# Tiles of split weights that begin at eight places of SBUF modulo 512 bytes instead of one

## The chip, the core and the metric

The kernel runs on one core of a Trainium2 chip. The metric is the device time of one execution in microseconds (us). A core has a matrix engine (TensorE: PE for its matmuls, PEld for the loads of its stationary operand), a vector engine (DVE), an activation engine (ACT), GpSimd (POOL), a queue engine (SP) and 16 DMA engines. They share SBUF, a memory of 128 partitions; a tile of `[128, n]` floats takes 4n bytes at one address in every partition. All addresses below are bytes within a partition.

## The reference

A trunk of two layers over 256 tokens of width 1024, in float32. Each layer adds half a SwiGLU (width 2816), an attention mixer and half a second SwiGLU, each on an RMS-normed input:

```python
h = rms_norm(x, ffn1_norm[layer])
x = x + 0.5 * swiglu(h, ffn1_w_gate[layer], ffn1_w_up[layer], ffn1_w_down[layer])
h = rms_norm(x, mix_norm[layer])
x = x + even_mixer(...)   # layer 0: global and windowed attention;  layer 1: odd_mixer, a neighbourhood
h = rms_norm(x, ffn2_norm[layer])
x = x + 0.5 * swiglu(h, ffn2_w_gate[layer], ffn2_w_up[layer], ffn2_w_down[layer])
```

A last norm follows. Nearly all of the work is products of 256 rows with large weight matrices, each of which is read once.

## The kernel before

**Split products.** A float32 weight W is split into a high part, W rounded to float32r, and a low part, W minus the high part. The activations are split likewise. A product is then three matmuls in float32r (`mm`, L474 to L476): activation high by weight high, activation high by weight low, activation low by weight high. The activation (a 128 by 128 block of `th`, `tl`, `g_h`, `g_l` and the like) is the stationary operand, which a load (LDWEIGHTS, shown as PEld) brings in ahead of each matmul; the weight part (512 columns of `hi` or `lo`) is the moving operand that streams past it. A row `s<-hi,th` is thus a matmul into the PSUM bank `s`, with `hi` moving and `th` stationary.

**The supply of weights.** Weights arrive by DMA in the tiles `raw` (three buffers of 8192 bytes). ACT makes the high part of up to 1024 columns (`high_part`, L482, `hi<-raw`), DVE then the low part (`low_part`, L485, `lo<-raw,hi`: two inputs in SBUF). `supply` (L422 on) takes a pair of tiles for that from the pool `wp`, which holds seven `hi` and seven `lo`, so that up to seven splits lie ready ahead of the matmuls. Splits of sums of weights (`shi`, `slo`, kind "sum") have buffers of their own in the phase pool, three each.

**The order of the work** is written out by the kernel itself: each matmul calls `tick`, which steps waiting tasks and supplies a split when a rate says that it is due. The change doesn't touch any of this.

**Places in SBUF.** Pools lie behind each other: `one` (x, the transposed activations `th` and `tl`, constants), `raw`, `wp`, `two` (small tiles), and behind these the pools of each phase (`g_h`, `g_l`, `shi`, `slo`, attention tiles). The tiles that matmuls and splits read are whole multiples of 512 bytes, and `one` begins so that they start at 128 modulo 512: x at 4224, `th` at 12416, `raw` at 28800, the seven `hi` at 53376 + 4096 n, the seven `lo` at 82048 + 4096 n. The first small tile of `two` is `mhalf`, a constant of `FILLER` columns of which at most eight are read; at 96 columns its end is at 111104, and with it the phase pools begin at 113280, which is 128 modulo 512 as well. A block of a stationary operand is 512 bytes and a moving one 2048 bytes, so that every matmul of 512 columns reads both of its operands from 128 modulo 512 on. That place is called the common one here.

Of the kernel before, what the change touches and what calls it, by code (L numbers as in the profile page):

```python
# [9 lines left out]
F32 = mybir.dt.float32  # L10
F32R = mybir.dt.float32r
# [7 lines left out]
P = 128  # L19
# [103 lines left out]
AHEAD_START = 8  # L123
FIRST = [1, 1, 2, 2, 2]

FILLER = 96
HALF = [slice(0, HD), slice(HD, P)]

ROW = 224
# [6 lines left out]
class Split:  # L136
# [3 lines left out]
    def __init__(self, raw, uses, last=False, narrow=False, kind="wp", then=None):  # L140
        self.raw, self.last, self.narrow, self.kind, self.then = raw, last, narrow, kind, then
        n = raw.shape[1]
        self.left = sum(uses[i % len(uses)] for i in range(n))
        self.parts, self.made = None, 0
# [64 lines left out]
class Trunk:  # L209
# [4 lines left out]
    def __init__(self, ctx, tc, a, out):  # L214
        self.ctx, self.tc, self.nc, self.a, self.out = ctx, tc, tc.nc, a, out
        pool = lambda name, bufs, **kw: ctx.enter_context(tc.tile_pool(name=name, bufs=bufs, **kw))
        self.one = pool("one", 1)
        self.ph = None
        self.raw = pool("raw", RAWS)
        self.wp = pool("wp", FIT["wp"])  # L220

        self.two = pool("two", 2)
        self.acc = pool("acc", 1, space=PSUM)
        self.n = 0
        self.rate = RATE[0]
        self.tasks, self.last, self.last_v = [], [], [[], []]
        self.units, self.whole, self.queue, self.due, self.half = self.plan(), [], [], 0, None
        self.live = {kind: 0 for kind in FIT}
        self.ahead = len(FIRST) - RAWS

        self.hts = {}

    def name(self, s):
        self.n += 1
# [185 lines left out]
    def supply(self):  # L420

        self.low()  # L422
        if not self.whole:
            return
        split = self.whole[0]
        _, a, w = split.raw.shape
        if split.parts is None:
            if split.kind == "wp":
                split.parts = [self.wp.tile([P, 2, 512], F32R, tag=n, name=self.name(n)) for n in ("hi", "lo")]
            else:  # L430
                split.parts = [self.t([P, 2, 512], n, FIT["sum"], F32R) for n in ("shi", "slo")]
            split.parts = [t[:, :a, :w] for t in split.parts]
            self.live[split.kind] += 1
        sl = slice(split.made, split.made + split.step())
        self.high_part(split.parts[0][:, sl], split.raw[:, sl])
        split.made = sl.stop
        self.half = (split, sl)
        if split.made == a:
            self.whole.pop(0)
# [1050 lines left out]
    def run(self):  # L1490
# [7 lines left out]
        def warm(n):  # L1498
            for _ in range(n):
                nc.tensor.matmul(nothing, zero16[:, :P], zero16, start=True, stop=True)  # L1500

        self.warm = warm
        warm(WARM)
        self.mhalf = self.little([P, FILLER], "mhalf")
        nc.gpsimd.memset(self.mhalf, -0.5)
# [73 lines left out]
```

## Time and profile before

| what | value |
|---|---|
| time, median of two runs | 935.4 us (935.3 to 935.5) |
| profiled execution, its own time | 935.71 us |
| its span, first to last instruction | 933.7 us |
| granted TensorE clock, mean | 0.999 |
| busy: PE, DVE, ACT, POOL | 921.5, 773.4, 675.9, 92.6 us |
| instructions on PE | 4405 |
| `hi` by ACT (L482) | 372 instructions, 320.1 us |
| `lo` by DVE (L485) | 372 instructions, 377.7 us |

The span is the stretch in which instructions ran; the execution's own time is 2.0 us longer. The end of a matmul in the profile is modelled and overlaps the next one, so the length of a matmul in a row (0.39 us) is not what it costs. What a stream of matmuls costs is read from the distance between their starts.

### The profile page before, as it was taken

The numbers are of one execution on the slowest core, as the hardware profiler recorded it, in microseconds if no ns is written. First come the engines' busy times: TensorE is split into PE (matmuls) and PEld (weight loads), VectorE is DVE, ScalarE is ACT, GpSimd is POOL, SyncE is SP. The second block draws the span as 40 slices with busy tenths as digits, with TensorE's granted clock in tenths as the row PEclk, the third lists the DMA queues.
The fourth block names the chain that finished last, engine by engine and source line by source line (L and its number), as shares of the span: only waits on it lengthen the run. The fifth ranks groups of instructions, "written<-read, shape, count | busy, mean of one in ns | idle before, by whom it ended". The sixth has DMA issues, their size and how long they took to land.

```text
span 933.7 us, 12374 instructions
## 1 busy us (share of the span) xinstructions
PE 921.5 (99%) x4405; PEld 754.3 (81%) x4405; DVE 773.4 (83%) x1198; ACT 675.9 (72%) x1084; POOL 92.6 (10%) x152
## 2 busy tenths in 40 slices
PE   9999999999999999999999999999999999999997
PEld 6887888877778888888888888888878888888885
DVE  6799679778868889799878888978867696977898
ACT  7778876467777778885657879657777586778853
POOL 1300000064420000000100000008030000000001
PEclk9999999999999999999999999999999999999999
DMA  8857865644327577757466787566434367588651
GB/s 297 283 172 256 244 213 184 218 142 109 112 92 231 173 237 236 233 191 265 156 193 211 216 278 207 225 210 200 155 99 159 105 204 225 168 265 254 164 212 53
DMA packets 129341, 183.14 MB, mean 196 GB/s; under 512 B 50688, under 2 KB 63744, under 8 KB 129280
## 3 DMA queue, kind: packets, MB, share of 16 engines
q1 hardware_dynamic: 128704, 181.58, 61.8%
q8 instruction: 34, 0.56, 0.2%
q10 hardware_dynamic: 576, 0.79, 0.2%
q14 instruction: 27, 0.22, 0.1%
HBM read 169.76 MB, written 1.05 MB: 183 GB/s over the span
## 4 chain that ended last, share of the span: by engine, by line
PE 88%; DVE 7%; ACT 3%; issue 1%; POOL 0%; POOLq 0%; ACTq 0%; DVEq 0%
PE s L476 13%; PE s L475 13%; PE s L474 12%; PE pj L474 12%; PE pj L475 11%; PE pj L476 11%; DVE lo L485 3%; PE o L474 2%; PE o L476 2%; PE o L475 2%; PE o L1053 2%; PE tp L1130 1%; ACT hi L482 1%; PE tp L530 1%; PE tp L474 1%
## 5 line engine op out<-in xcount | busy, mean ns | idle before, releaser
L485 DVE TENSOR_TENSOR lo<-raw,hi 128x1024 fp32r<-128x1024 f32 (+1 forms) x372 | 377.7, 1034 | 81.8 <-ACT hi L482 80.2
L482 ACT ACTIVATE hi<-raw 128x1024 fp32r<-128x1024 f32 (+1 forms) x372 | 320.1, 892 | 53.9 <-PE s L476 12.6
L474 PE MATMUL s<-hi,th 128*128 128x512 f32 x378 | 148.1, 392 | 0.0
L475 PE MATMUL s<-lo,th 128*128 128x512 f32 x378 | 147.2, 389 | 0.2 <-DVE lo L485 0.2
L476 PE MATMUL s<-hi,tl 128*128 128x512 f32 x378 | 147.2, 390 | 0.0
L474 PE MATMUL pj<-hi,th 128*128 128x512 f32 x366 | 146.2, 399 | 0.0
L475 PE MATMUL pj<-lo,th 128*128 128x512 f32 x366 | 143.2, 391 | 0.6 <-DVE lo L485 0.4
L476 PE MATMUL pj<-hi,tl 128*128 128x512 f32 x366 | 142.8, 390 | 0.0
L475 PEld LDWEIGHTS s<-lo,th 128*128 128x128 f32 x378 | 71.0, 188 | 15.0 <-DVE lo L485 0.5
L476 PEld LDWEIGHTS s<-hi,tl 128*128 128x128 f32 x378 | 70.9, 188 | 14.9
L474 PEld LDWEIGHTS s<-hi,th 128*128 128x128 f32 x378 | 71.0, 188 | 14.5
L475 PEld LDWEIGHTS pj<-lo,th 128*128 128x128 f32 x366 | 68.9, 188 | 15.2 <-DVE lo L485 2.6
L476 PEld LDWEIGHTS pj<-hi,tl 128*128 128x128 f32 x366 | 68.7, 188 | 14.5
L474 PEld LDWEIGHTS pj<-hi,th 128*128 128x128 f32 x366 | 68.8, 188 | 14.0 <-issue 1.0
L494 POOL TENSOR_TENSOR rstd<-var,mhalf 128x1 f32<-128x1 f32 (+2 forms) x16 | 17.1, 1070 | 586.6 <-ACT th L515 309.7
L563 ACT COPY turned<-glu 128x1024 uint16<-128x1024 uint16 (+1 forms) x48 | 60.2, 1253 | 13.2 <-DMA glu<-turned 13.2
L559 ACT COPY turned<-glu 128x1024 uint16<-128x1024 uint16 (+1 forms) x48 | 46.3, 965 | 24.1 <-DVE glu L797 16.3
L482 ACT ACTIVATE shi<-raw 128x1024 fp32r<-128x1024 f32 x28 | 29.6, 1059 | 32.7 <-DVE raw L398 23.0
L474 PE MATMUL s<-hi,g_h 128*128 128x512 f32 (+1 forms) x134 | 52.5, 392 | 0.0
L476 PE MATMUL s<-hi,g_l 128*128 128x512 f32 (+1 forms) x134 | 52.0, 388 | 0.0
L475 PE MATMUL s<-lo,g_h 128*128 128x512 f32 (+1 forms) x134 | 52.0, 388 | 0.0
L482 ACT ACTIVATE shi<-two 128x1024 fp32r<-128x1024 f32 x28 | 29.6, 1058 | 23.8 <-DVE two L398 23.7
(350 smaller groups left out, 1657.3 us busy)
## 6 DMA issues: line engine op xcount, KB each, us to landing
raw<-in_ffn_w_down SPq DMA_DIRECT2D x44, 1024.0 KB, 5.1
raw<-in_ffn_w_up SPq DMA_DIRECT2D x28, 1024.0 KB, 5.1
raw<-in_ffn_w_gate SPq DMA_DIRECT2D x26, 1024.0 KB, 5.3
raw<-in_ffn_w_gate SPq DMA_DIRECT2D x35, 512.0 KB, 4.2
raw<-in_ffn_w_up SPq DMA_DIRECT2D x32, 512.0 KB, 5.2
raw<-in_odd_w_qkv SPq DMA_DIRECT2D x12, 1024.0 KB, 5.2
raw<-in_even_w_in SPq DMA_DIRECT2D x4, 1024.0 KB, 5.1
raw<-in_even_w_out SPq DMA_DIRECT2D x8, 512.0 KB, 5.7
```

Of the source, the lines that this page charges most:

```text
L474: mm(ps, h, wh, start=first, stop=False)
L475: mm(ps, h, wl, start=False, stop=False)
L476: mm(ps, l, wh, start=False, stop=last)
L482: self.nc.scalar.activation(hi, src, AF.Copy)
L485: self.nc.vector.tensor_tensor(lo, src, hi.bitcast(F32), op=ALU.subtract)
L494: nc.gpsimd.tensor_tensor(r[:, :n], v[:, :n], self.mhalf[:, :n], op=ALU.pow)
L530: nc.tensor.transpose(tb[:, j * P : (j + 1) * P], self.x[tt][:, b * P : (b + 1) * P], self.ident)
L559: self.nc.scalar.copy(planes.rearrange("p (h c) -> p h c", h=2), back.rearrange("p (c h) -> p h c", h=2))
L563: self.nc.scalar.copy(planes.rearrange("p (c h) -> p h c", h=2), back.rearrange("p (h c) -> p h c", h=2))
L1053: self.nc.tensor.matmul(O[64 * s : 64 * s + 64, i * P : i * P + P], v(b0 + i, s, kc), pT[s][:, i, kc, :], start=(kc == 0), stop=(kc == 1),)
L1130: nc.tensor.transpose(tb[:, o : o + P], p[:, i, kc * P : kc * P + P], self.ident)
```

## The change: what it does

`hi` tiles get eight columns more than are used (1032 floats, 4128 bytes), so that each of the seven begins 32 bytes later modulo 512 than the one before it. Between the last `hi` and the first `lo` lies a new tile `apart` of 32 bytes, to which nothing is written; the seven `lo` tiles keep their size. `mhalf` shrinks from 96 to 32 columns, by as many bytes as the others have gained (7 x 32 + 32 = 256), so that everything behind it stays where it was.

| tile | before, modulo 512 | after, modulo 512 |
|---|---|---|
| `hi`, the seven | 128 each | 128, 160, 192, 224, 256, 288, 320 |
| `lo`, the seven | 128 each | 384 each |
| `raw`, x, `th`, `tl`, `g_h`, `g_l`, `shi`, `slo` | 128 | 128 |

The instructions of every engine, their order, their sizes and their waits are the same, apart from the memset of `mhalf`, which writes 32 columns for 96.

```diff
-FILLER = 96
+FILLER, STEP = 32, 8
...
-        self.hts = {}
+        self.hts, self.apart = {}, []
...
             if split.kind == "wp":
-                split.parts = [self.wp.tile([P, 2, 512], F32R, tag=n, name=self.name(n)) for n in ("hi", "lo")]
+                hi = self.wp.tile([P, 1024 + STEP], F32R, tag="hi", name=self.name("hi"))
+                if not self.apart:
+                    self.apart.append(self.wp.tile([P, STEP], F32, tag="apart", name=self.name("apart"), bufs=1))
+                lo = self.wp.tile([P, 2, 512], F32R, tag="lo", name=self.name("lo"))
+                split.parts = [hi[:, :1024].rearrange("p (a w) -> p a w", a=2), lo]
             else:
                 split.parts = [self.t([P, 2, 512], n, FIT["sum"], F32R) for n in ("shi", "slo")]
```

## The prediction

> **What bounds the kernel now.** I read the page first, its busy times and its chain of work, then PE's waits, then the starts of single matmuls in the timeline. From the page:
>
> ```profile
> span 933.7 us, 12374 instructions
> PE 921.5 (99%) x4405; PEld 754.3 (81%) x4405; DVE 773.4 (83%) x1198; ACT 675.9 (72%) x1084; POOL 92.6 (10%) x152
> ...
> PE 88%; DVE 7%; ACT 3%; issue 1%; POOL 0%; POOLq 0%; ACTq 0%; DVEq 0%
> PE s L476 13%; PE s L475 13%; PE s L474 12%; PE pj L474 12%; PE pj L475 11%; PE pj L476 11%; DVE lo L485 3%; PE o L474 2%; PE o L476 2%; PE o L475 2%; PE o L1053 2%; PE tp L1130 1%; ACT hi L482 1%; PE tp L530 1%; PE tp L474 1%
> ```
>
> PE has work nearly all the time and the chain lies on it for 88%. Of the instructions whose addresses change, DVE's `lo` holds 3% of the chain and ACT's `hi` 1%. What PE itself waited for, longest first:
>
> ```profile
> PE o L1500 <- DVE zeros L1494: 1.4, 1, 1.4
> ...
> PE pj L475 <- DVE lo L485: 0.4, 2, 0.2
> PE o L475 <- DVE lo L485: 0.3, 2, 0.2
> ...
> PE s L475 <- DVE lo L485: 0.2, 1, 0.2
> ```
>
> PE's waits for `lo` sum to 0.9 us (its weight loads add a few more), so that the supply of weights is in time. What is left to gain is the distance between matmuls. Timeline of a stretch inside a feed-forward stage (start, length, engine, line):
>
> ```profile
> 399.36 1.05 ACT L482 ACTIVATE shi<-two 128x1024 fp32r<-128x1024 f32 x1
> ...
> 399.58 0.39 PE L474 MATMUL s<-hi,g_h 128*128 128x512 f32 x1
> 399.58 0.19 PEld L475 LDWEIGHTS s<-lo,g_h 128*128 128x128 f32 x1
> 399.81 0.39 PE L475 MATMUL s<-lo,g_h 128*128 128x512 f32 x1
> 399.81 0.19 PEld L476 LDWEIGHTS s<-hi,g_l 128*128 128x128 f32 x1
> ...
> 400.49 0.39 PE L475 MATMUL o<-lo,g_h 128*128 128x512 f32 x1
> ...
> 401.17 0.39 PE L475 MATMUL pj<-lo,g_h 128*128 128x512 f32 x1
> ...
> 401.25 0.62 ACT L559 COPY turned<-glu 128x512 uint16<-128x512 uint16 x1 [0.85 <-DVE g_l L485]
> 401.39 0.39 PE L476 MATMUL pj<-hi,g_l 128*128 128x512 f32 x1
> ```
>
> From 399.58 to 401.39 there are eight distances in 1.81 us, 0.226 us each. ACT was at work until 400.41 and idle from then to 401.25 (its row gives 0.85 us of idle time); the three distances from 400.49 to 401.17, in that gap, are 0.227 us each. A busy neighbour thus costs PE nothing here. The next stationary load starts together with the running matmul: both operands are read at once, and both from the common place.
>
> Matmuls of 384 columns, near the end:
>
> ```profile
> 924.91 0.33 PE L474 MATMUL s<-hi,g_h 128*128 128x384 f32 x1
> ...
> 925.95 0.22 PE L474 MATMUL tp<-hi,g_h 128*128 128x128 f32 x1
> ```
>
> Six distances lie in 1.04 us, 0.1733 us each. Against 0.2265 us for 512 columns, 128 columns cost about 53 ns, 0.415 ns a column, and about 14 ns of every matmul don't depend on its length. That is all that a better place could save on PE: a stream that met another's bank again and again along its way would cost by the column.
>
> **The change part by part.** All durations are of the one profiled execution, which took 935.71 us by itself and 933.7 us as a span; the median of the two timed runs is 935.4 us, 0.3 us less, and the sum is made on that.
>
> *Matmuls on moved tiles.* Counted in the built program, 3696 matmuls have 512 columns; 2240 read `hi`, 1120 `lo`, 336 `shi` or `slo`. One `hi` tile in seven keeps its place (316 matmuls), so 2240 - 316 + 1120 = 3044 read from a new one. Before, none of the 3696 had its operands at different places, so the price has to be bounded. The nearest row in which both reads go on at once is a run of transposes of `x` (moving: the identity, stationary: a block of `x`, both from the common place):
>
> ```profile
> 448.55 0.60 PE L530 MATMUL tp<-mats,x 128*128 128x128 f32 x4
> 448.55 0.35 PEld L530 LDWEIGHTS tp<-mats,x 128*128 128x128 f32 x3
> ...
> L530 PE MATMUL tp<-mats,x x80: 270/272/328, 181.2 to 754.0; 128*128 128x128 f32 x80
> ```
>
> Four of them take 0.60 us to the end of the last, whose length is 0.272, so three distances are 0.33 us: 109 ns. At twice the 0.415 ns (these are plain float32) 128 columns are 106 ns, so that only some 3 ns are left over, with the loads beside them. If meeting at one place cost a fixed 14 ns, it should stand here too. I therefore hold the 14 ns to belong to a float32r matmul and not to its place, and take 0. The bounds: below, 14 - 3 = 11 ns less for each of 3044, -33 us; above, the slowest steady stretch of such matmuls, in the even mixer:
>
> ```profile
> 215.50 0.39 PE L475 MATMUL pj<-lo,th 128*128 128x512 f32 x1
> ...
> 216.42 0.39 PE L476 MATMUL pj<-hi,tl 128*128 128x512 f32 x1
> ```
>
> Four distances in 0.92 us, 230 ns or 3.5 ns over the usual, with single ones of 0.24 (10 ns over): +11 us, at the farthest +30 us.
>
> *ACT's and DVE's splits.* Minimum, median and maximum in ns, of the tiles that move (two sizes mixed) and of those that stay (one size):
>
> ```profile
> L482 ACT ACTIVATE hi<-raw x372: 609/1044/1105, 6.2 to 915.2; 128x1024 fp32r<-128x1024 f32 x102, 128x512 fp32r<-128x512 f32 x84
> L485 DVE TENSOR_TENSOR lo<-raw,hi x372: 670/1217/1435, 6.9 to 916.5; 128x1024 fp32r<-128x1024 f32 x102, 128x512 fp32r<-128x512 f32 x84
> ...
> L482 ACT ACTIVATE shi<-raw x28: 1044/1062/1067, 53.8 to 910.9; 128x1024 fp32r<-128x1024 f32 x28
> L485 DVE TENSOR_TENSOR slo<-raw,shi x28: 1217/1220/1227, 54.8 to 912.0; 128x1024 fp32r<-128x1024 f32 x28
> ```
>
> From the smallest `lo` of 512 columns (670) to the median of 1024 (1217) the difference is 547 ns for 512 columns, about 1.07 ns a column, though both inputs and the output lie at the same place: no sign that two streams get in each other's way. A row whose places do differ says the same:
>
> ```profile
> L1142 DVE TENSOR_TENSOR t<-pj,gtab x10: 280/282/692, 225.5 to 238.5; 128x128 f32<-128x128 f32 x8, 128x512 f32<-128x512 f32 x2
> ...
> L1142 DVE TENSOR_TENSOR t<-pj,gtab 128x128 f32<-128x128 f32 x8 | 1.8, 281 | 0.0
> ```
>
> The eight of 128 columns write the four quarters of a head's 64 columns (`times(t2[:, :, o], ...)`), which begin 0, 64, 128 and 192 bytes behind the tile's start. Their smallest is 280 and their mean 281, so place moves DVE by no more than a few nanoseconds. So 0 for both. Bounds, on the chain's share alone (3% and 1% of 933.7, 28 and 9 us): all `lo` as long as the longest (1435 against 1217, 18%) and all `hi` at 1105 against 1044 (6%) give +5.6 us; at best each becomes as short as the shortest of its size (1044 against 1062, 1.7%, and 1217 against 1220, 0.2%), which gives -0.2 us. What covers such growth is the seven splits that lie ready; without that cover, PE would wait for each `lo` directly.
>
> The Trainium skill, "SBUF — State Buffer", section "Who interferes with whom", says that engines get in each other's way only at the ports that DVE and GpSimd share, and that PE and ACT never wait for anyone. PE's distances above agree with it. For ACT the rows leave it open (1044 to 1067 for one size in fixed places). By the rule alone the sum is 0 as well.
>
> *`mhalf`.* Its memset is one instruction at the start:
>
> ```profile
> L1505 POOL MEMSET mhalf<- x1: 177/177/177, 0.7 to 0.7; 128x96 f32 x1
> ```
>
> It can become 0.1 us shorter at most, and it runs while PE waits for DVE's zeros. 0.
>
> Sum: 935.4 + 0 + 0 + 0 = 935 us.
>
> **The rivals.** *Faster: the 14 ns are a collision of the two reads.* Each matmul would lose up to 11 ns where its moving operand begins elsewhere: 3044 x 11 ns = 33 us, 902 us. For it: every matmul in the trace has both operands at the same place, so the trace can't refute it. Against it: the transposes, and that the reads run at different speeds (2048 bytes against 512 in one matmul), so that wherever they begin the one must pass the other. It decides from 18.7 / 3044 = 6.1 ns a matmul. The Trainium skill, "TensorE: Matmul & The Clock Gate", section "Back-to-back issue gap", gives N / 2.4 + 2.5 ns for a stream, 216 ns at 512 columns, where this trace has 226.5; by it some 10 ns here would be foreign to a matmul, which would favour this case.
>
> *Slower: streams that begin off the common place cost PE.* Now both reads start in step and never vary; moved apart, or begun at an odd multiple of 32 bytes, a moving read might be held up more often, as some matmuls in the mixers are. At 7 ns a matmul (between the 3.5 and the 10 of the mixer's rows) it is 3044 x 7 = 21 us, 957 us. The point is again 6.1 ns. For it: the mixers show that distances above 226 ns exist. Against it: they stand only where matmuls of other shapes are mixed in.
>
> *No change, but DVE becomes later.* In the stretch with the densest DVE (busy us of PE, PEld, DVE, ACT and POOL; then PE, PEld and DVE on `lo` alone):
>
> ```profile
> 370.00:440.00 70.00, 70.00 (x311) 57.96 (x310) 61.62 (x76) 52.42 (x65) 0.00 (x0) 1.00 0.72 238
> 370.00:440.00 70.00, 35.36 (x92) 17.08 (x91) 32.78 (x29) 1.00 0.72 238
> ```
>
> Of 70 us DVE works 61.62, 32.78 of them on `lo`. `lo` would have to grow by 8.38 / 32.78 = 26% before DVE had no slack here; the longest row allows 18%. So this stays inside the bound of +6 us, 941 us.
>
> *The change does nothing that it says* is excluded as to the places, which the built program has as the table shows; that they don't matter is the forecast.
>
> **How the numbers follow.** A measurement of this kernel is taken to tell 2% (18.7 us) from no change. No change to speak of, with the splits' bounds and up to 3 ns a matmul on either side: 0.83, of which 0.05 for a later DVE. The collision that goes: 0.10. The moved streams that cost: 0.07. The likeliest case's own range is 935 - 0.2 - 9 to 935 + 5.6 + 9, 926 to 950; since an effect of 3 ns on every matmul is already unlikely and the upper bounds don't add up at once, I cut its upper end to 946 and give the lower end to 922, towards the likelier rival. Outside lie then the two rivals and a little of the rest, 0.2.
>
> **What would show it.** Right: the distance in the feed-forward stages stays 0.226 us, `hi` and `lo` keep their medians of 1044 and 1217, the span stays within some us of 933.7. The faster rival shows as distances of 0.215 to 0.220 on `lo` matmuls and on six `hi` tiles in seven, with the 384 columns at 0.162; the slower one as 0.23 and more, different from tile to tile; a later DVE as more than 0.9 us of PE's waits for `lo`. A changed distance would make the prediction wrong, for nothing else has the size.

## The result: slower by 1.4%, outside the range

The changed kernel takes 948.66 us (948.5 to 948.83) against 935.4 us: a ratio of 1.0142, 95% interval 1.0098 to 1.0185, 13.3 us. The profiled execution took 948.83 us, its span is 946.8 us, 13.1 us longer than before. The page after:

```profile
span 946.8 us, 12374 instructions
PE 935.1 (99%) x4405; PEld 754.9 (80%) x4405; DVE 774.1 (82%) x1198; ACT 677.1 (72%) x1084; POOL 91.6 (10%) x152
...
PE 88%; DVE 6%; ACT 3%; issue 1%; DMA 0%; POOL 0%; POOLq 0%; ACTq 0%; DVEq 0%
```

PE is still the bound, with 13.6 us more of busy time; DVE and ACT are as they were. Their splits have not moved either (L489 and L486 are L485 and L482 of before):

```profile
L486 ACT ACTIVATE hi<-raw x372: 612/1044/1107, 6.4 to 928.2; 128x1024 fp32r<-128x1024 f32 x102, 128x512 fp32r<-128x512 f32 x84
L489 DVE TENSOR_TENSOR lo<-raw,hi x372: 673/1215/1431, 7.1 to 929.6; 128x1024 fp32r<-128x1024 f32 x102, 128x512 fp32r<-128x512 f32 x84
```

Nor does PE wait more for `lo`; it was 0.9 us before:

```profile
PE o L479 <- DVE lo L489: 0.3, 2, 0.2
```

What has grown is the distance between matmuls. The same matmuls of a feed-forward stage in the timeline after, two stretches of it:

```profile
402.03 0.40 PE L478 MATMUL s<-hi,g_h 128*128 128x512 f32 x1
402.26 0.39 PE L479 MATMUL s<-lo,g_h 128*128 128x512 f32 x1
...
404.13 0.39 PE L478 MATMUL pj<-hi,g_h 128*128 128x512 f32 x1
...
409.70 0.39 PE L478 MATMUL pj<-hi,g_h 128*128 128x512 f32 x1
...
411.74 0.40 PE L478 MATMUL o<-hi,g_h 128*128 128x512 f32 x1
```

From 402.03 to 404.13 there are nine distances of 0.233 us. From 409.70 to 411.74 there are nine of 0.227 us, as before the change: there the trace, set beside the program, has a `hi` tile at 128 modulo 512, the one that did not move, with its `lo` at 384. Over the trace, the distances behind matmuls of 512 columns (those under 260 ns, some 3575 in each) have a mean of 227.36 ns before and 231.25 ns after, 3.9 ns more. 3575 x 3.9 ns = 13.9 us: that is the whole loss. In a window of 170 us without mixers (busy us and count of PE), before and after:

```profile
440.00:610.00 170.00, 170.00 (x759) 1.00 0.69 213
```

```profile
440.00:610.00 170.00, 170.00 (x745) 1.00 0.66 207
```

Fourteen matmuls fewer fit into it, 1.8%. This count is used below for the other kernels.

### The profile page after: what moved, and what is told of

It reads as the page before. It is cut to its first block, busy times and chain, and to the rows that moved or that the text cites. A ratio compares the mean times of both kernels' runs of the same rounds, so it can differ in the third digit from the quotient of the medians.

```text
span 946.8 us, 12374 instructions
## 1 busy us (share of the span) xinstructions
PE 935.1 (99%) x4405; PEld 754.9 (80%) x4405; DVE 774.1 (82%) x1198; ACT 677.1 (72%) x1084; POOL 91.6 (10%) x152
## 4 chain that ended last, share of the span: by engine, by line
PE 88%; DVE 6%; ACT 3%; issue 1%; DMA 0%; POOL 0%; POOLq 0%; ACTq 0%; DVEq 0%
PE s L480 13%; PE s L478 13%; PE s L479 13%; PE pj L478 12%; PE pj L480 12%; PE pj L479 12%; DVE lo L489 3%; PE o L478 2%; PE o L479 2%; PE o L480 2%; PE o L1057 2%; PE tp L1134 1%; PE tp L534 1%; ACT hi L486 1%; PE tp L478 1%
## 5 line engine op out<-in xcount | busy, mean ns | idle before, releaser
L489 DVE TENSOR_TENSOR lo<-raw,hi 128x1024 fp32r<-128x1024 f32 (+1 forms) x372 | 377.8, 1033 | 85.6 <-ACT hi L486 84.8
L486 ACT ACTIVATE hi<-raw 128x1024 fp32r<-128x1024 f32 (+1 forms) x372 | 321.1, 892 | 69.0 <-PE s L480 24.8
L486 ACT ACTIVATE shi<-raw 128x1024 fp32r<-128x1024 f32 x28 | 29.7, 1059 | 37.5 <-DVE raw L398 19.4
L486 ACT ACTIVATE shi<-two 128x1024 fp32r<-128x1024 f32 x28 | 29.6, 1056 | 20.7 <-DVE two L398 20.6
```

The source lines that it names most:

```text
L486: self.nc.scalar.activation(hi, src, AF.Copy)
L489: self.nc.vector.tensor_tensor(lo, src, hi.bitcast(F32), op=ALU.subtract)
```

## Experiments

Three theories were set against each other. **A**: the place of the moving operand against the place of the stationary one counts. **B**: successive moving operands must begin at the same place. **C**: neighbours (ACT, DVE, the DMA engines) get in PE's way.

### Matmuls alone

A kernel of its own, with PE alone at work on zeros: 60 matmuls a segment, 14 tiles of moving and 8 of stationary operands, in the kernel's order. Each segment gives the distances of its stationary and its moving operands from the common place.

```diff
+        out.append((f"con{c}", 512, lambda k, c=c: (0, step(c))))
...
+        out.append((f"hl{h}{l}", 512, lambda k, h=h, l=l: (0, step(l if k % 3 == 1 else h))))
...
+        out.append((f"st{c}", 512, lambda k, c=c: (step(c), 0)))
...
+        out.append((f"both{c}", 512, lambda k, c=c: (step(c), step(c))))
```

> Matmuls alone, on zeros: the trunk is left out, and no other engine works beside PE. Segments of 60 matmuls of 512 columns in float32r; conX has all moving operands X x 32 bytes behind the place of the stationary ones (a = 0, b = 32, c = 64 and so on, i = 256), hlXY has high parts at X and low parts at Y in the kernel's order high, low, high; stX moves the stationary ones, bothX both alike, walk steps the place by 32 every six matmuls. Theory A (what costs is the place of the moving operand against the stationary one): cona, botha and bothc 226.7 ns from start to start, conb to cong and stX some 231. Theory B (what costs is that successive moving operands begin at different places): every conX and stX 226.7, hlXY with X other than Y about 231. Theory C (neighbours on ACT, DVE and the DMA engines do it): every segment 226.7. In A and B hlai may be free, since one tile after the change ran at 226.7 with its low part 256 off.

The timeline of PE merges a segment into one row: its start, and the time to the end of its last matmul.

```profile
46.32 13.83 PE L71 MATMUL cona<-buf 128*128 128x512 f32 x60
...
60.27 14.21 PE L71 MATMUL conb<-buf 128*128 128x512 f32 x60
...
74.60 13.96 PE L71 MATMUL conc<-buf 128*128 128x512 f32 x60
...
103.02 14.15 PE L71 MATMUL cone<-buf 128*128 128x512 f32 x60
...
117.29 14.27 PE L71 MATMUL conf<-buf 128*128 128x512 f32 x60
...
131.68 14.21 PE L71 MATMUL cong<-buf 128*128 128x512 f32 x60
...
146.01 13.82 PE L71 MATMUL coni<-buf 128*128 128x512 f32 x60
...
188.55 13.82 PE L71 MATMUL hlai<-buf 128*128 128x512 f32 x60
...
230.94 14.21 PE L71 MATMUL hlab<-buf 128*128 128x512 f32 x60
...
345.14 14.21 PE L71 MATMUL stc<-buf 128*128 128x512 f32 x60
...
373.75 13.83 PE L71 MATMUL sti<-buf 128*128 128x512 f32 x60
...
387.70 13.84 PE L71 MATMUL bothc<-buf 128*128 128x512 f32 x60
```

With 0.39 us off for the last one and 59 distances, cona has 227.8 ns, and 226.7 in its second half, once the first few matmuls are past. At 32 bytes of distance (conb) it is 234.2, at 64 (conc) 230.0, at 128 (cone) 233.2, at 160 (conf) 235.3, at 192 (cong) 234.2, at 256 (coni) 227.6 again. Moving the stationary operand by 64 costs as much as moving the other one by 192, which is the same difference modulo 256 (stc and cong, 14.21 both); moving it by 256 costs nothing (sti), and moving both by 64 nothing (bothc). C is not needed: the cost is there with no neighbour at work. B is out as the only cause: in conb to cong all moving operands begin at one place. A holds, with a period of 256 bytes. But it is not all: in hlab two operands of three are at the common place and only the third is 32 bytes off, and the segment takes as long as conb (14.21), where all are off. The seven pairs of the changed kernel, hlai, hlbi, hlci, hldi, hlei, hlfi, hlgi, take 13.82, 14.08, 14.21, 14.15, 13.97, 14.15 and 14.26 us, in the mean 0.26 us or 4.4 ns a matmul more than cona; on the 3360 matmuls with `hi` and `lo` that is 15 us, where 13.1 were lost.

### One part of the change at a time

Low parts alone, 256 bytes behind the common place, all `hi` at it:

```diff
-FILLER = 96
+FILLER = 32
...
+                hi = self.wp.tile([P, 2, 512], F32R, tag="hi", name=self.name("hi"))
...
+                    self.apart.append(self.wp.tile([P, 64], F32, tag="apart", name=self.name("apart"), bufs=1))
+                lo = self.wp.tile([P, 2, 512], F32R, tag="lo", name=self.name("lo"))
```

> High parts stay at the common place, low parts 256 bytes behind it as in the change. Theory A and theory B with a period of 256: as before, 935 us. With a period of 512: a third of the matmuls is off, +4 us or more, 940 us (A), and every neighbour differs, 948 us (B).

935.86 us beside 935.73, ratio 1.0001 (0.9992 to 1.0011), and 759 matmuls in the window: free, as A and B with a period of 256 had it.

The steps of the high parts alone (`lo` first in the pool, at the common place, then `hi` with eight columns more, `FILLER` 40):

```diff
+                lo = self.wp.tile([P, 2, 512], F32R, tag="lo", name=self.name("lo"))
+                hi = self.wp.tile([P, 1024 + 8], F32R, tag="hi", name=self.name("hi"))[:, :1024].rearrange("p (a w) -> p a w", a=2)
```

> High parts step by 32 bytes as in the change, low parts stay at the common place. Theory A: 1924 of 3696 matmuls are off by 4 ns, 943 us. Theory B: six triples of seven alternate between places, as in the change, 947 us.

948.45 us, ratio 1.0136 (1.0120 to 1.0151): all of the loss comes with the steps. A's number of 943 assumed that only the 1924 moved matmuls pay. In the trace the `lo` between them, at 128 themselves, pay too: the distances behind them (those under 260 ns) have a mean of 231.0 ns, against 227.3 in the kernel before. So an alternation costs the neighbour as well, as in hlab, and B, though not the cause of conb to cong, has a share.

### All split weights by 64, by 32, and everything by 64

```diff
-FILLER = 96
+FILLER = 80
...
+                    self.apart.append(self.wp.tile([P, 16], F32, tag="apart", name=self.name("apart"), bufs=1))
+                hi = self.wp.tile([P, 2, 512], F32R, tag="hi", name=self.name("hi"))
```

> High and low parts all begin 64 bytes behind the common place, so that successive moving operands agree, but not with the stationary ones. Theory A: 3360 matmuls are off, 948 us or more. Theory B: 935 us.

942.54 us, ratio 1.0073 (1.0058 to 1.0088), 751 matmuls in the window. Between both numbers: B alone would be 935. A's direction is right; its 4 ns were those of the mixture. The segment conc has 2.2 ns for 64 bytes in its second half (228.9), and 3360 x 2.2 = 7.4 us, where 6.8 were measured. With that price the run with 32 bytes was forecast (8 columns for 16, `FILLER` 88):

> As the run with all split weights 64 bytes behind the common place, with 32 bytes. By theory A with the distances of the streams alone (233.4 ns at 32 bytes against 226.7): 3360 matmuls x 6.7 ns = 22.5 us, 958 us; the same sum gave 3360 x 2.2 = 7 us for 64 bytes, where 6.8 were measured. By a theory in which any place off the common one costs the same, about 942 us as with 64 bytes.

953.94 us beside 935.77, ratio 1.0192 (1.0175 to 1.0209), 740 matmuls in the window: 18.2 us of the 22.5. The price of A depends on the distance. The sum is too high by 4.3 us. Some 2.6 us of that come from its start: in the kernel before, the distances behind `hi` and `lo` have a mean of 227.4 ns, not 226.7, mostly because those in the mixers are longer, and 3360 x 0.76 ns = 2.6 us. The rest is open.

Then everything, `th`, `tl`, `g_h` and the rest too, 64 bytes later:

```diff
+        one.tile([P, 16], F32, tag="apart", name="apart")
         zeros = one.tile([P, 512], F32, tag="sq", name="zeros")
```

> Every tile, stationary operands included, begins 64 bytes later, so that the common place is 192 and nothing moves against anything else. Theory A: 935 us, as before. If the place itself counts (a grid of 128 bytes, say): about 942 us, as with the split weights alone moved by 64.

935.75 us beside 935.52, ratio 1.0003 (0.9993 to 1.0013), 759 matmuls. The place by itself costs nothing, only the distance does.

### Finer distances, and which two reads

The same kernel with moving operands 4 to 252 bytes off, with alternating places, and with fewer columns:

```diff
+        out.append((name, 512, lambda k, d=d: (0, d)))
...
+        out.append(("own" + c, 512, lambda k, d=d: (d * (k % 2), d * (k % 2))))
+        out.append(("lead" + c, 512, lambda k, d=d: (d * (k % 2), d * ((k + 1) % 2))))
...
+        out.append((name, n, lambda k: (0, 0)))
+        out.append((name + "c", n, lambda k: (0, 64)))
```

> Matmuls alone on zeros, the trunk left out. Moving operands 4 to 252 bytes behind the place of the stationary ones, 60 matmuls each. Theory A (the two reads of PE get in each other's way, by their distance modulo 256): distances between starts of 226.7 ns at 0 and 229 to 234 elsewhere, 4 to 12 bytes nearer to 226.7; if some place lies under 226.7, the kernel before can be beaten by it. Own and lead alternate the places of the stationary operand: in own each moving operand begins where its own stationary one did, in lead where the next one does, which is loaded meanwhile. If the reads that run at the same time collide, lead is at 226.7 and own is above; if the place of a matmul's own two operands counts, the other way round. Narrow, mid and wide have 128, 256 and 384 columns, the letter c 64 bytes of distance: mid 120 and midc 118 as in the first such run, wide 173 and widec 1 to 3 ns from it.

```profile
46.73 13.82 PE L68 MATMUL same<-buf 128*128 128x512 f32 x60
...
60.67 14.42 PE L68 MATMUL four<-buf 128*128 128x512 f32 x60
...
89.55 13.95 PE L68 MATMUL twelve<-buf 128*128 128x512 f32 x60
...
289.80 13.83 PE L68 MATMUL twofiftytwo<-buf 128*128 128x512 f32 x60
...
303.74 14.11 PE L68 MATMUL ownc<-buf 128*128 128x512 f32 x60
...
317.97 14.21 PE L68 MATMUL leadc<-buf 128*128 128x512 f32 x60
...
332.30 14.40 PE L68 MATMUL owne<-buf 128*128 128x512 f32 x60
...
346.81 14.02 PE L68 MATMUL leade<-buf 128*128 128x512 f32 x60
...
360.95 6.86 PE L68 MATMUL narrow<-buf 128*128 128x128 f32 x60
...
367.99 6.86 PE L68 MATMUL narrowc<-buf 128*128 128x128 f32 x60
...
375.02 7.40 PE L68 MATMUL mid<-buf 128*128 128x256 f32 x60
...
382.55 7.28 PE L68 MATMUL midc<-buf 128*128 128x256 f32 x60
...
389.95 10.62 PE L68 MATMUL wide<-buf 128*128 128x384 f32 x60
...
400.69 10.63 PE L68 MATMUL widec<-buf 128*128 128x384 f32 x60
```

Four bytes behind cost 10 ns a matmul (four against same), four before (252) nothing, twelve 2 ns; that small distances be cheap, as A had it, is wrong, and no place of the seventeen lies under 226.7. Own and lead settle nothing: all four are above same, with 64 bytes lead is the worse and with 128 own. Which matmul's stationary operand a moving one has to agree with is left open.

The price holds for 512 columns. At 384 columns 64 bytes of distance cost nothing (wide and widec, both 173.3 ns in the second half; 1 to 3 ns were expected), at 128 columns nothing either (narrow and narrowc, 111.7 ns), and at 256 columns they save 2.2 ns: 120.0 ns in mid, 117.8 in midc, and the same in the first such kernel. So equal places are not the best for every length. The lengths also give the price of a column: from 384 to 512 columns it is 53.3 ns for 128, so that 512 columns by themselves would take 213.3 ns, and at equal places 13.3 ns are left over at 256, 384 and 512 columns alike.

### What the reads collide on

The access patterns are replaced: still reads the moving columns with a step of 0, four reads 128 of them four times, weight reads the stationary columns with a step of 0, every reads each second moving column; in alt only the moving operand alternates, between 0 and 64 bytes.

```diff
+                rows = bass.AP(rows.tensor, first, [rows.ap[0], *w])
...
+                    weight = bass.AP(weight.tensor, weight.offset, [weight.ap[0], *at_w])
```

> Matmuls alone on zeros, the trunk left out, 512 columns, to see what the two reads collide on. Still: all 512 moving columns are the same address, four: the same 128 columns four times, weight: all 128 stationary columns are the same address, swap: the two halves of the moving operand in the other order, every: each second column; letters a, c, e are 0, 64, 128 bytes of distance; alt: only the moving operand alternates between 0 and 64. If every matmul pays a fixed 32 cycles and the rest is a collision of two reads that walk through the same banks: weighta to weighte and stilla to stille differ little from each other (nothing walks on one side), at 226.7 ns or below. If the 32 cycles are collisions too: still or weight falls under 226.7, towards 216. Four repeats 512 bytes and should be as the plain stream: 226.7, 229 and 232. Alt is above 226.7 by theory B as by theory A.

```profile
74.20 13.20 PE L74 MATMUL stilla<-buf 128*128 128x512 f32 x60
...
87.52 13.85 PE L74 MATMUL foura<-buf 128*128 128x512 f32 x60
...
101.48 14.11 PE L74 MATMUL weighta<-buf 128*128 128x512 f32 x60
...
129.66 13.19 PE L74 MATMUL stillc<-buf 128*128 128x512 f32 x60
...
157.06 14.12 PE L74 MATMUL weightc<-buf 128*128 128x512 f32 x60
...
241.51 27.44 PE L74 MATMUL every<-buf 128*128 128x512 f32 x60
```

A moving operand that stays at one address takes 217 ns a matmul at any distance (216.3 in the second half), 10 ns less than the best stream that walks. So the 13.3 ns that float32r matmuls pay over their columns are not a fixed price of theirs: 10 of them go when the moving read doesn't walk through memory. Four takes as long as the plain stream (foura 13.85). Alt takes 14.07 us, more than conc (13.96), where all moving operands are 64 bytes off: again an alternation has a price of its own. With the stationary read on one address instead (weighta, weightc), the distance no longer matters, but each matmul takes 232.5 ns. One picture is that the moving read and the load of the next stationary operand meet in the same part of SBUF, and that at 512 columns equal places give the fewest meetings. That the two reads act on each other is shown by the segments in which only their difference counts. How they do is not: a load from one address makes the stream slower, not faster, and no stream of float32r matmuls without loads was run, so that the 10 ns may also be a price of the moving walk alone.

Whether another walk meets less often was the last question:

> Matmuls alone on zeros, the trunk left out, 512 columns, to see whether another way through the operands collides less than the kernel before does. Back: the moving columns are read from the last to the first; two and quad: the 128 stationary columns lie 2 or 4 floats apart; letters a to h are 0 to 224 bytes of distance in steps of 32. If stalls are collisions of two walks, the speed and direction of the walks change their number: some of these should fall under 226.7 ns (towards the 216 of a moving operand that doesn't walk), and a kernel with such operands would beat both. If 226.7 is the least that two walking reads can do, all of them lie at 226.7 or above.

```diff
+        out.append(("back" + c, [[-1, 512]], None, at(d)))
+        out.append(("two" + c, plain, [[2, 128]], at(d)))
...
+        out.append(("quad" + c, plain, [[4, 128]], at(d)))
```

```profile
46.57 13.83 PE L72 MATMUL same<-buf 128*128 128x512 f32 x60
...
60.52 14.22 PE L72 MATMUL backa<-buf 128*128 128x512 f32 x60
...
247.01 14.02 PE L72 MATMUL twog<-buf 128*128 128x512 f32 x60
...
304.30 14.73 PE L72 MATMUL quadc<-buf 128*128 128x512 f32 x60
...
333.68 13.12 PE L78 MATMUL halfa<-buf 128*128 128x512 bf16 x60
346.63 13.11 PE L78 MATMUL halfc<-buf 128*128 128x512 bf16 x60
```

None of 19 is under same; the nearest is twog with 14.02. Equal places are not enough for that, either: backa, read from the other end, takes 14.22. For matmuls of 512 columns none of the places and walks tried with a moving operand of 512 different columns beats the places of the kernel before; some, like 252 bytes, equal them. (halfa and halfc are bfloat16 operands at distances of 0 and 64 bytes.)

## Why the prediction was wrong

**What bounds the kernel, the splits, `mhalf`**: right. PE stayed the bound with 88% of the chain, ACT's and DVE's medians are 1044 and 1215 against 1044 and 1217, and PE's waits for `lo` did not grow.

**Matmuls on moved tiles** is the step that failed: "I therefore hold the 14 ns to belong to a float32r matmul and not to its place, and take 0". The term is not 0 but +13.9 us, 3.9 ns a matmul. What a float32r matmul of 512 columns pays over its columns goes with the difference between the places of its two operands: 13.3 ns where they are equal, 20 ns at 32 bytes. And 10 of the 13.3 ns go with a moving operand that stands still, so they are not the matmul's own. The step drew on two observations that do not carry it. The transposes, 109 ns each, were taken to have only 3 ns to spare. But float32r matmuls of 128 columns, with 53 ns of columns, take 111.7 ns too, and the same 64 bytes apart (narrow, narrowc): something else holds up so short a matmul, so its distance can't show a price of place. With that the 3 ns of the lower bound, and its 11 ns, have nothing under them. And that the 14 ns don't depend on the number of columns was taken to exclude meetings "again and again along its way". They don't depend on it (13.3 ns at 256, 384 and 512 columns), and still they go with the walk of the moving read and grow with its place.

The whole uniformity of the trace was a warning: 3696 matmuls, all at one distance, can say nothing on another. The prediction said so under the bounds, and its bound above, from the mixers' 230 ns (+11 us), was nearly the result. That is luck: in the mixers the operands lay at equal places, so their 230 ns have another cause, which no run tests.

**The slower rival** had the right sign and the right condition ("moved apart, or begun at an odd multiple of 32 bytes, a moving read might be held up more often"); whether it is holding up that makes the distances longer is not shown. Its price of 7 ns a moved matmul was too high: 13.3 us on its 3044 matmuls are 4.4 ns, so that 957 us became 948.7. (Those that didn't move pay too, so that it is 3.9 ns over all.) "Odd multiple of 32" was not the point, since the pure distances of 128 and 192 bytes (233.2 and 234.2 ns) cost about as much as 32 does (234.2). It stayed under the 6.1 ns of a change by 2%, so the change is within 2%, for a reason that the forecast did not have.

**The faster rival** had the two reads as the cause, which the runs bear out as far as their places go, and the wrong sign: at 512 columns no place tried is faster than equal ones. Its remark that some 10 ns were foreign to the matmul fits the segments still, where 10 ns go. The rule that it leaned on is in the Trainium skill, "TensorE: Matmul & The Clock Gate", section "Back-to-back issue gap": N / 2.4 + 2.5 ns, which the section calls the gap of isolated matmuls, while it gives about 131 ns at 512 columns for a stream with loads. Here the formula is met by a stream with loads, the bfloat16 segments: (13.12 - 0.38) / 59 = 215.9 ns a matmul in halfa and 215.8 in halfc, and no stream came near 131 ns. The other rule, of the Trainium skill, "SBUF — State Buffer", section "Who interferes with whom", says that PE never waits on anyone. It leaves out what the runs show: PE's distances change with the places of its own two operands.

**The range** ended at 946 although its parts reached 950: the prediction took 3 ns on every matmul to be unlikely. 3.9 ns on every matmul is what came.

## What to carry to other kernels

In a stream of float32r matmuls of 512 columns with a stationary load each, let moving and stationary operands begin at the same place modulo 256 bytes; a pad of 32 bytes behind each `hi` tile cost 1.4%, and a common shift of the split weights by 32 bytes 1.9%. For other lengths measure it: at 256 columns 64 bytes of distance were faster. Where PE is the bound, read the distances between starts, not the lengths, and compare them with what the columns alone take, 53.3 ns for 128 here. Where every instance in a trace shares one value of what a change varies, the trace has no price for it: measure a stream of it alone, or keep the bounds wide.

## What had not been expected of the hardware

- The period is 256 bytes, not 512: 256 bytes of distance are free (coni, sti, the kernel with `lo` 256 behind).
- The cost isn't smooth: 236.7 ns at 4 bytes (second half of the segment), 228.9 at 12, 226.7 at 252.
- It depends on the length: 64 bytes of distance cost 2.2 ns at 512 columns, nothing at 384, and save 2.2 ns at 256.
- A moving operand of every second float32 column takes twice as long (every, 27.44 us for 60, against 13.83).
- No cost of neighbours was seen on PE: in the feed-forward stages of the kernel before, with ACT, DVE and the DMA engines at work, the usual distance is the 0.227 us that PE alone takes in the streams (226.7 ns).
